# A third sum buffer, sum loads in SyncE's queue, and a VectorE subtraction for all late fourth sums, in an FFN made of seven-product blocks

## The chip, the cores and the metric

The kernel runs on one core of one Trainium2 chip. The metric is device time in microseconds (us) of one execution. The engines are named as in the profile: PE (TensorE), DVE (VectorE), ACT (ScalarE), POOL (GpSimd) and SP (SyncE, which here only issues DMAs).

## The reference

Two layers of a "macaron" encoder over 512 tokens and 16 learned meta tokens, model width 1024, FFN width 2816, float32. The change lies in the FFNs:

```python
def swiglu(x, w_gate, w_up, w_down):
    return (jax.nn.silu(x @ w_gate) * (x @ w_up)) @ w_down
...
for l in range(DEPTH):                       # DEPTH = 2
    h = h + 0.5 * swiglu(rmsnorm(h, norm_gains[l, 0]), ffn_w_gate[l, 0], ...)
    h = h + mixer(rmsnorm(h, norm_gains[l, 1]), ...)   # gated linear attention + softmax attention
    h = h + 0.5 * swiglu(rmsnorm(h, norm_gains[l, 2]), ffn_w_gate[l, 1], ...)
return rmsnorm(h, final_norm)[:, N_META:]
```

There are four FFNs in all, each with 11 pairs of 128 hidden features.

## The kernel before

**Products.** The matrix products of the FFNs are cut into 2 × 2 blocks and made by the scheme that takes seven products instead of eight. Every product is an "op" of one block of weights, 128 × 1024 (512 KB), against one half of the columns: 8 block tiles, each with three matmuls of 264 columns, so 24 matmuls. Three of the products (1, 2 and 4) use stored blocks, called 11, 12 and 22. Four (7, 6, 5 and 3) use sums of blocks that the kernel makes itself: s3 = 21 − 11, s2 = 22 + s3, s1 = 21 + 22, s4 = s2 − 12. The order of the products in a pair is 1, 2, 5, 6, 7, 4, 3 with changes where neighbours interleave.

**Splitting.** Every block is taken apart for the matmuls: ACT casts it to the short float format (`whi`, L259) and DVE subtracts that from the block for the rest (`wlo`, L260). The matmul needs both.

**Stages.** The 11 pairs (numbers 0 to 10) go in groups of 4, 4 and 3. A pair is the gate and up product (matmuls on line L566, the activation on L412, and L610, L620 that make its operands). After each of the first two groups stands a *down set*, two *quads* (numbered 11, 12 and 13, 14) that multiply the group's hidden values by `w_down` with the same seven products (matmuls L680), added into `h` by DVE (L688). A quad's product reads accumulators that an earlier addition must have emptied. The third group's down product is made in the plain way. The pairs that begin after a set are pair 4 and pair 8.

**Loads and sums.** The stored blocks are loaded by `block` (L193) into a pool of three raw buffers, in SP's queue. A sum begins in one of two pools: s3 and s4 in the "long" pool (three buffers), s2 and s1 in the "short" one (two buffers). s2 and s1 begin as a load of block 22 or 21 by the same `block`, but in POOL's queue, and then a DMA that accumulates (`add`, L203, always in POOL's queue) adds the other summand. s3 begins as a negated copy of block 11 by ACT (`negative`, L198). s4 is made in one of two ways: as a negated copy of block 12 by ACT (L198), to which POOL's queue accumulates s2; or, when `late` is true, by one DVE subtraction (L228) of block 12 from s2. For that the raw buffer of block 12 is kept (`self.kept`) until product 6's split has been made. `late` holds for pairs 2 to 10; the quads and the first two pairs take the first way.

**Order.** `make` prepares operands four ops ahead of PE and `fetch` loads nine ahead. The scheduler places the instructions of each engine by its own estimate of times; on the chip each engine, and each DMA queue's issuing engine, then goes through its list in order and waits at every entry for its semaphores.

Of the kernel before, what the change touches and what calls it, by code (L numbers as in the profile page):

```python
# [143 lines left out]
NPAIR = FF // P // 2  # L144
# [21 lines left out]
class Weights:  # L166
# [21 lines left out]
    def block(self, f, i, name, pool=None, tag="raw"):  # L188

        w = (pool or self.raw).tile([P, SLAB], F32, tag=tag, name=f"w{name}_{f[0]}{f[1]}_{i}")  # L190
        first = f + (i, name) == (0, 0, 0, "11")
        for a in np.split(np.arange(SLAB), 2 if first else 1):
            (self.nc.gpsimd if pool else self.nc.sync).dma_start(w[:, a[0] : a[-1] + 1], self.dram(f, i, name)[:, a[0] : a[-1] + 1])  # L193
        return w

    def negative(self, f, i, name, w):
# [8 lines left out]
    def sums(self, f, i, product, w):  # L205


        got = self.summed
        if product == "1":
            s3 = self.negative(f, i, "s3", w)  # L210
            self.add(s3, self.dram(f, i, "21"))
            s2 = self.block(f, i, "22", self.short, "wsb")
            self.add(s2, s3)
            got[f, i, "7"], got[f, i, "6"] = s3, s2
        if product == "12"[(f, i) in OPENING]:
            s1 = self.block(f, i, "21", self.short, "wsb")
            self.add(s1, self.dram(f, i, "22"))
            got[f, i, "5"] = s1
        late = 2 <= i < NPAIR
        if product == "2" and not late:  # L220
            s4 = self.negative(f, i, "s4", w)
            self.add(s4, got[f, i, "6"])
            got[f, i, "3"] = s4
        if product == "2" and late:
            self.kept = w
        if product == "6" and late:
            s4 = self.long.tile([P, SLAB], F32, tag="wsa", name=f"s4_{f[0]}{f[1]}_{i}")
            self.nc.vector.tensor_tensor(s4, w, self.kept, ALU.subtract)  # L228
            got[f, i, "3"] = s4
# [67 lines left out]
def build(tc, ctx, xt, wts, win, par, w2, const, umask, out):  # L297
# [17 lines left out]
    def open_pools(side, psum=(), **bufs):  # L315
        made[0] += 1
        out = {}
        for n, b in bufs.items():
            space = dict(space=bass.MemoryType.PSUM) if n in psum else dict(side=side)
            out[n] = tc.alloc_tile_pool(name=f"{n}_{made[0]}", bufs=b, reuse_waits="tile", **space)  # L320
        slots.update(out)
        return out
# [218 lines left out]
    def ffn(l, f, norm, done, following):  # L541

        x, rs, up, n = norm.x, None, None, live[0]
        w = n // 2
        pools = open_pools("left", psum=("s2",), c=4, s2=2)
        made, hid, sums, raw, sets = {}, {}, {}, {}, {}
        risen = iter(range(KC))

# [540 lines left out]
        norm.pools = open_pools("right", **{"x": dict(x=16), "xc": dict(xc=8)}[kind])  # L1089

    def block_pools():
        pools = open_pools("left", wsa=3, wsb=2)
        W.long, W.short = pools["wsa"], pools["wsb"]
        return pools

# [89 lines left out]
    def finish_chunk(c):  # L1185
        fin.square(c)
        gain(c, slice(0, SEQ))

    def ending(sums, operand, rs):

        table("abs_reciprocal_sqrt_and_small")
# [44 lines left out]
    first = Norm(G_NORM)  # L1236
    operand_pools(first, "xc")
    bp = [block_pools()]
    nc.sync.dma_start(h(1), xt[:, 1])
    first.pair(0)  # L1240
# [15 lines left out]
    for l in range(DEPTH):  # L1256
        a, b, c = norms[3 * l : 3 * l + 3]
        ffn(l, 0, a, b.chunk, lambda: operand_pools(b, "x"))
        close_pools(bp.pop())
        mixer(l, b, c.chunk_of_pair, lambda: (operand_pools(c, "xc"), bp.append(block_pools())))  # L1260
        if l < DEPTH - 1:
            d = norms[3 * l + 3]
            ffn(l, 1, c, d.pair_of, lambda: operand_pools(d, "xc"))
        else:
            ffn(l, 1, c, None, lambda: None)
# [72 lines left out]
```

## Time and profile before

| what | value |
|---|---|
| runs of the kernel | 2270.09, 2262.52, 2267.75 us; median 2267.75 |
| the profiled execution | 2280.39 us, its span 2278.6 us |
| mean granted clock of TensorE | 0.989 |
| busy in the span | PE 2188.9 us, DVE 1685.8, ACT 1262.7, POOL 246.1 |
| the four FFNs | about 0 to 405, 797 to 1145, 1142 to 1548, 1914 to 2279 us |
| DMA issues by L193 on POOL | 120, 576 ns of the engine each |
| DMA issues by L203 on POOL | `s<-win` 60, `w<-s` 60, `w<-win` 60, `s<-w` 24 |

A timeline row gives the start, the duration, engine, line, operation, what it writes and reads, and in brackets the idle time before it with what ended that. In the chain of waits a row is a piece of the chain that ended last: start, duration, and who held it. `w` stands for a block or short sum, `s` for a long sum, `win` for the stored blocks in memory, `ss` for an accumulator. A row of the waits names who waited for whom, the time in all, how often, and the longest.

### The profile page before, as it was taken

The page shows a single profiled execution, that of the slowest core. Times are in us where ns is not written, and L with a number is a line of the kernel's source. Part 1 is how long each engine was busy: PE and PEld are TensorE (multiplying, and loading weights), DVE is VectorE, ACT ScalarE, POOL GpSimd, SP SyncE. Part 2 cuts the span into 40 slices and gives each one's busy share as a digit, 9 for nine tenths or more (in the row PEclk, how much of TensorE's full clock was granted, in tenths as well). Part 3 has the DMA queues.
Part 4 walks back from the last instruction along what each step waited for, and adds up shares of the span by engine and source line. Part 5 has one row for each costly group of instructions (what it writes and reads, how often), then busy time and mean ns, then how long its engine had stood idle before and what let it go on. Part 6 is the DMA issues. An engine that isn't in the chain of part 4 may idle for free.

```text
span 2278.6 us, 40100 instructions
## 1 busy us (share of the span) xinstructions
PE 2188.9 (96%) x16506; PEld 2088.3 (92%) x16506; DVE 1685.8 (74%) x2607; ACT 1262.7 (55%) x1831; POOL 246.1 (11%) x328
## 2 busy tenths in 40 slices
PE   6989999999999999999999899999999999999998
PEld 6989999989999999998999898998888888999997
DVE  7776867586886678667788768575878767786867
ACT  7545545354785565454575455454547846555553
POOL 1211110000000011111012111100000001121110
PEclk9999999999999999999999999999999999999999
DMA  8877873212113477777668777832121135887871
GB/s 241 217 198 185 203 195 106 77 54 66 47 38 112 129 189 187 204 192 202 175 148 208 201 193 178 201 114 86 56 74 47 47 121 136 216 213 213 204 204 65
DMA packets 94951, 338.68 MB, mean 149 GB/s; under 512 B 10544, under 2 KB 12976, under 8 KB 94768
## 3 DMA queue, kind: packets, MB, share of 16 engines
q0 software_dynamic: 46656, 169.89, 33.9%
q1 hardware_dynamic: 46160, 163.73, 21.2%
q8 instruction: 130, 2.13, 0.4%
q10 hardware_dynamic: 1952, 2.50, 0.3%
q14 instruction: 53, 0.43, 0.1%
HBM read 289.94 MB, written 2.10 MB: 128 GB/s over the span
## 4 chain that ended last, share of the span: by engine, by line
PE 60%; DMA 13%; DVE 12%; issue 8%; ACT 6%; POOL 1%; SPq 0%; DVEq 0%; POOLq 0%; ACTq 0%
PE ss L566 24%; PE mm L433 14%; DMA w<-win 10%; PE ss L433 9%; PE ss L680 4%; DVE wlo L260 3%; PE sm L433 2%; DMA w<-s 2%; ACT whi L259 1%; PE sm L1041 1%; DMA s<-w 1%; PE ss L1016 1%; POOL w L203 1%; ACT s L198 1%; PE sm L1057 1%
## 5 line engine op out<-in xcount | busy, mean ns | idle before, releaser
L566 PE MATMUL ss<-xc,whi 128*128 128x264 f32 (+1 forms) x4928 | 905.6, 285 | 25.6 <-ACT whi L259 13.4
L566 PEld LDWEIGHTS ss<-xc,whi 128*128 128x128 f32 x4928 | 767.1, 189 | 30.8 <-ACT whi L259 14.3
L566 PE MATMUL ss<-xc,wlo 128*128 128x264 f32 (+1 forms) x2464 | 702.1, 285 | 3.7 <-DVE wlo L260 3.7
L260 DVE TENSOR_TENSOR wlo<-w,whi 128x1024 fp32r<-128x1024 f32 (+1 forms) x301 | 365.5, 1217 | 155.6 <-ACT whi L259 155.4
L566 PEld LDWEIGHTS ss<-xc,wlo 128*128 128x128 f32 x2464 | 466.3, 189 | 5.8 <-DVE wlo L260 5.8
L259 ACT CAST whi<-w 128x1024 fp32r<-128x1024 f32 (+1 forms) x301 | 313.0, 1047 | 143.1 <-DMA w<-win 34.0
L433 PE MATMUL mm<-x,whi 128*128 128x264 f32 (+1 forms) x1712 | 385.3, 315 | 0.0
L433 PEld LDWEIGHTS mm<-x,whi 128*128 128x128 f32 x1712 | 279.2, 189 | 16.5 <-issue 1.0
L680 PE MATMUL ss<-g,whi 128*128 128x264 f32 (+1 forms) x1280 | 250.9, 294 | 29.2 <-DVE h L688 17.2
L433 PE MATMUL mm<-x,wlo 128*128 128x264 f32 (+1 forms) x856 | 266.7, 316 | 0.0
L680 PEld LDWEIGHTS ss<-g,whi 128*128 128x128 f32 x1280 | 206.8, 196 | 35.9 <-ACT whi L259 19.5
L259 ACT CAST whi<-raw 128x1024 fp32r<-128x1024 f32 x126 | 132.1, 1049 | 164.4 <-PE mm L433 103.0
L570 ACT COPY c<-ss 128x528 f32<-128x528 f32 (+1 forms) x132 | 78.5, 595 | 224.3 <-PE ss L566 224.1
L260 DVE TENSOR_TENSOR wlo<-raw,whi 128x1024 fp32r<-128x1024 f32 x126 | 153.9, 1222 | 59.3 <-ACT whi L259 58.5
L680 PE MATMUL ss<-g,wlo 128*128 128x264 f32 (+1 forms) x640 | 186.1, 291 | 0.7 <-DVE wlo L260 0.7
L193 POOL DMA_DIRECT2D w<-win x120 | 69.1, 576 | 1079.9 <-DVE x L422 731.2
L260 DVE TENSOR_TENSOR wlo<-s,whi 128x1024 fp32r<-128x1024 f32 x120 | 146.5, 1221 | 43.5 <-ACT whi L259 43.4
L433 PEld LDWEIGHTS mm<-x,wlo 128*128 128x128 f32 x856 | 160.1, 189 | 8.5 <-issue 0.7
L433 PE MATMUL ss<-g,whi 128*128 128x264 f32 (+2 forms) x900 | 166.2, 299 | 0.0
L259 ACT CAST whi<-s 128x1024 fp32r<-128x1024 f32 x120 | 126.1, 1051 | 22.7 <-PE ss L680 15.3
L433 PEld LDWEIGHTS ss<-g,whi 128*128 128x128 f32 x900 | 131.7, 188 | 5.3
L680 PEld LDWEIGHTS ss<-g,wlo 128*128 128x128 f32 x640 | 125.3, 196 | 1.0 <-DVE wlo L260 1.0
(266 smaller groups left out, 3430.8 us busy)
## 6 DMA issues: line engine op xcount, KB each, us to landing
w<-win POOLq DMA_DIRECT2D x180, 512.0 KB, 6.1
w<-win SPq DMA_DIRECT2D x179, 512.0 KB, 5.4
raw<-wts SPq DMA_DIRECT2D x126, 512.0 KB, 3.3
s<-win POOLq DMA_DIRECT2D x60, 512.0 KB, 7.6
w<-s POOLq DMA_DIRECT2D x60, 512.0 KB, 5.2
s<-w POOLq DMA_DIRECT2D x24, 512.0 KB, 7.7
h<-xt SPq DMA_DIRECT2D x3, 528.0 KB, 8.7
out<-h ACTq DMA_DIRECT2D x4, 256.0 KB, 2.3
```

The source lines that it names most:

```text
L193: (self.nc.gpsimd if pool else self.nc.sync).dma_start(w[:, a[0] : a[-1] + 1], self.dram(f, i, name)[:, a[0] : a[-1] + 1])
L198: self.nc.scalar.activation(t, w, AF.Copy, scale=-1.0)
L203: self.nc.gpsimd.dma_start(t, src, accum_op=ALU.add)
L259: nc.scalar.copy(hi[:, cs], w[:, cs])
L260: nc.vector.tensor_tensor(lo[:, cs], w[:, cs], hi[:, cs].bitcast(F32), ALU.subtract)
L433: TE.matmul(acc.half[i][:width], lhs, rhs[:, acc.spans[i]], start=first, stop=last)
L566: TE.matmul(acc[:, j], a[:, j, k], b[:, at], start=bool(begin and k == 0 and i == 0), stop=k == len(x) - 1 and i == 2, skip_group_check=no ...
L570: W.behind = S.copy(part(st, q), acc).ins
L680: TE.matmul(acc[:, j], a[:, j, k], xs[b][:, k], start=bool(begin and k == 0 and i == 0), stop=k == 3 and i == 2, skip_group_check=not begin)
L1016: TE.matmul(s[:n, i, :HF], lhs, kh[:, hs], start=True, stop=False)
L1041: TE.transpose(tp[:, j * w + u * n : j * w + (u + 1) * n], pr[:n, (2 * c2 + j) * P : (2 * c2 + j + 1) * P], ident[:n, :n])
L1057: TE.matmul(o[:, :w], vw, ph, start=i == 0, stop=False)
```

## The change

It has three edits:

1. `block` loads into the short pool go in SP's queue too: 120 loads, 60 of block 22 (s2) and 60 of block 21 (s1). The accumulating DMAs stay in POOL's queue.
2. `late` holds for the quads too. In the 16 quads (four per FFN) s4 is made by the DVE subtraction, 52 in all instead of 36; 16 negations on ACT and 16 accumulations in POOL's queue go away (24 `s<-w` become 8). The quads' raw block 12 is kept until its s2 has been split.
3. The short pool has three buffers instead of two.

```diff
     def block(self, f, i, name, pool=None, tag="raw"):
         ...
         for a in np.split(np.arange(SLAB), 2 if first else 1):
-            (self.nc.gpsimd if pool else self.nc.sync).dma_start(w[:, a[0] : a[-1] + 1], self.dram(f, i, name)[:, a[0] : a[-1] + 1])
+            self.nc.sync.dma_start(w[:, a[0] : a[-1] + 1], self.dram(f, i, name)[:, a[0] : a[-1] + 1])
         return w
...
     def sums(self, f, i, product, w):
         ...
-        late = 2 <= i < NPAIR
+        late = 2 <= i
...
     def block_pools():
-        pools = open_pools("left", wsa=3, wsb=2)
+        pools = open_pools("left", wsa=3, wsb=3)
         W.long, W.short = pools["wsa"], pools["wsb"]
         return pools
```

## The prediction

> **What bounds the kernel now.** I read the page's busy times first, then the waits of TensorE, then the six worst places in the timelines and in the chain of waits. TensorE is busy nearly all the time; the changed lines belong to POOL, SP and VectorE, so they can only be worth something where PE waits for them:
>
> ```profile
> PE 2188.9 (96%) x16506; PEld 2088.3 (92%) x16506; DVE 1685.8 (74%) x2607; ACT 1262.7 (55%) x1831; POOL 246.1 (11%) x328
> ...
> PE ss L680 <- DVE h L688: 18.5, 8, 4.3
> PE ss L566 <- ACT whi L259: 13.4, 4, 8.9
> ```
>
> The span is 2278.6 us, so PE is idle for 2278.6 − 2188.9 = 89.7 us. The longest item (us, times, longest) is a matmul of a down set, L680, that waits for a VectorE addition into `h`, L688. In the window of the last FFN alone the same item is small, so six of the eight waits, worth 18.5 − 1.3 = 17.2 us, are in the three FFNs before it (two sets each):
>
> ```profile
> PE ss L680 <- DVE h L688: 1.3, 2, 0.7
> ```
>
> What holds that addition is seen in the VectorE and PE timelines at the end of the first down set:
>
> ```profile
> 149.68 1.23 DVE L260 TENSOR_TENSOR wlo<-w,whi 128x1024 fp32r<-128x1024 f32 x1 [0.30 <-ACT whi L259]
> 156.80 1.23 DVE L228 TENSOR_TENSOR s<-w,w 128x1024 f32<-128x1024 f32 x1 [5.89 <-DMA w<-s]
> 157.94 0.70 DVE L688 TENSOR_TENSOR h<-h,ss 128x528 f32<-128x528 f32 x1
> ...
> 154.22 0.28 PE L680 MATMUL ss<-g,wlo 128*128 128x264 f32 x1
> 158.79 0.78 PE L680 MATMUL ss<-g,whi 128*128 128x264 f32 x2 [4.29 <-DVE h L688]
> ```
>
> VectorE takes its instructions in order. The subtraction L228 that makes the fourth sum of the next pair stands ahead of the addition, and it waits 5.89 us for its operand, the second sum (a DMA that accumulates, `w<-s`). PE's last product of the set needs the buffer that the addition reads, and stands still for 4.29 us. The wait also costs the clock. The window table puts the granted clock at 0.52 between 157 and 164, and the chain of waits gives the run of 24 matmuls behind each of the six stalls, beside a run at full speed:
>
> ```profile
> 157.00:164.00 7.00, 5.21 (x24) 5.24 (x25) 4.53 (x5) 0.87 (x1) 0.56 (x1) 0.52 1.02 252
> ...
> 158.79 5.37 PE ss L680 x24
> 164.16 10.86 PE ss L566 x89
> 292.31 4.70 PE ss L680 x24
> 930.29 4.47 PE ss L680 x24
> 1064.42 4.68 PE ss L680 x24
> 1299.78 4.68 PE ss L680 x24
> 1437.16 4.57 PE ss L680 x24
> ```
>
> 10.86/89 = 0.122 us a matmul; 24 take 2.93 us. The six runs take 28.47 us against 6 × 2.93 = 17.58: 10.9 us more. A set's end therefore costs 17.2 + 10.9 = 28.1 us in all six.
>
> **The change, part by part.** First the order on VectorE. Built, the changed program has at all eight set ends: `wlo` of the next pair's product 1, the addition L688, then L228. That order exists in the trace already, in the last FFN:
>
> ```profile
> 2041.49 0.69 DVE L688 TENSOR_TENSOR h<-h,ss 128x512 f32<-128x512 f32 x1 [0.60 <-PE ss L680]
> 2044.96 1.23 DVE L228 TENSOR_TENSOR s<-w,w 128x1024 f32<-128x1024 f32 x1 [2.78 <-DMA w<-s]
> ...
> 2029.87 17.24 PE ss L680 x143
> ```
>
> L228 still waits 2.78 us for its DMA there, yet PE runs on: 143 matmuls in 17.24 us, 0.121 each. So the stall goes, unless what stands behind L228 is late next. Behind it on VectorE is `wlo` of product 2. In the first set PE would end product 3 at 154.22 + 0.28 = 154.50, then run two products of 2.93 to 160.36. L228 takes until 157.94 − 156.80 = 1.14 before its successor starts, and `wlo` 1.22: L228 must start by 160.36 − 1.14 − 1.22 = 158.0. Before, PE restarts 158.79 − 156.80 = 1.99 after L228 starts, so the spare time of a set end is about 158.0 − 154.5 + 1.99 − stall = 5.5 − stall: 1.2 us at the first, and 5.5 − (17.2 − 4.29)/5 = 2.9 in the mean of the other five.
>
> Will the second sum come as early as now? The chain ahead of the first end, the release of its raw buffer in the changed kernel, and the issue groups (median us to landing):
>
> ```profile
> 133.18 7.60 DMA w<-win
> ...
> 140.86 1.07 ACT s L198
> ...
> 142.33 0.19 POOL s L203
> ...
> 143.49 5.83 DMA w<-win
> ...
> 149.37 0.63 issue
> 149.99 6.73 DMA w<-s
> ...
> 135.87 1.22 DVE L260 TENSOR_TENSOR wlo<-w,whi 128x1024 fp32r<-128x1024 f32 x1
> ...
> w<-win SPq DMA_DIRECT2D x179, 512.0 KB, 5.4
> s<-win POOLq DMA_DIRECT2D x60, 512.0 KB, 7.6
> w<-s POOLq DMA_DIRECT2D x60, 512.0 KB, 5.2
> ```
>
> Two effects oppose each other. The load at 143.49 is the second sum's own; it lands at 149.32, and the accumulation starts after it. With a third buffer and SP's queue it is issued some 20 us sooner and binds no longer. But the raw block of product 1 was issued at 133.18 because L198 had freed block 12; that block is now kept for the new subtraction, and the raw load waits for the `wlo` that ends at 137.09, 3.9 us later. From there, with medians: 137.1 + 5.4 + 0.1 + 1.47 (140.86 to 142.33) + 7.6 + 0.6 + 5.2 = 157.5, against 156.72 now. With 5.2 for the middle accumulation it is 155.1; with the chain's own 7.60 and 6.73 it is 161.2. I take 1.3 us for the first end (half way from 157.5 to the high end is 159.3, past 158.0), and none for the others, whose spare 2.9 holds the 0.8. Set ends: −28.1 + 1.3 = −26.8, bounds −28.1 and, at the high end, −11 (worked out below).
>
> By the Trainium skill, "TensorE: Matmul & The Clock Gate", Part 1, the clock falls to half after an idle window of about 3.4 us. By that rule alone only the first stall would cost the clock, and the set ends would hold 17.2 + 2.4 = 19.6 us. The trace disagrees: after 2.21 us of idle time (292.31) the 24 matmuls took 4.70, so the sum stays with the rows.
>
> The opening of the first FFN is the other place with a second sum that comes late:
>
> ```profile
> 37.77 6.64 DMA w<-win
> ...
> 45.08 4.84 DMA w<-s
> ...
> 51.04 0.80 PE L566 MATMUL ss<-xc,whi 128*128 128x264 f32 x2 [3.52 <-ACT whi L259]
> 52.30 0.59 PE L566 MATMUL ss<-xc,wlo 128*128 128x264 f32 x1 [0.46 <-DVE wlo L260]
> 52.30 7.77 PE ss L566 x41
> ...
> 30.25 1.22 POOL L203 DMA_DIRECT2D s<-win  x1
> ```
>
> That load had to wait for one of two buffers; now it goes in the first microseconds. What binds instead is the third sum's accumulation, issued at 30.25; at the 7.6 median it lands at 37.9, and the whole 3.52 + 0.46 + (7.77 − 41 × 0.122 = 2.77) = 6.75 us could go. The DMA engines are full in the opening, and one transfer sooner is another later, so the bounds are 0 and −6.75 (a loss is not excluded, but the moved load carries the bytes it carried), and I take half: −3.4.
>
> The sixteen new subtractions, and those next to them:
>
> ```profile
> L228 DVE TENSOR_TENSOR s<-w,w 128x1024 f32<-128x1024 f32 x36 | 43.9, 1221 | 39.5 <-DMA w<-s 39.5
> ...
> 110.72 1.23 DVE L260 TENSOR_TENSOR wlo<-w,whi 128x1024 fp32r<-128x1024 f32 x1 [2.64 <-ACT whi L259]
> ...
> 101.79 0.90 POOL L203 DMA_DIRECT2D w<-s  x1 [6.50 <-DMA w<-win]
> ```
>
> 16 × 1.22 = 19.5 us of VectorE. In the first three FFNs the first quad's stands in the hole of 2.64 us before 110.72, provided its second sum is there: its accumulation was issued at 101.79, and 5.2 later is 107.0. So 1.22 fits in 2.64, at no cost. In the last FFN it stands in the chain from the activation to the next operand, with no hole: 2 × 1.22 = 2.4 us if all shows, 0 if PE has work; I take 1.2. The second quad's eight stand between a `wlo` and the next, cost nothing while those are ahead of PE, and 8 × 1.22 = 9.8 at worst. Sixteen negations on ACT and sixteen accumulations leave POOL's queue; neither row is on PE's path at a set end, so nothing, save less DMA traffic. Moving 120 loads off POOL takes issue time from an engine that is 11% busy: nothing.
>
> Sum: −26.8 − 3.4 + 1.2 = −29.0 us. The profiled execution took 2280.39 us; by it the changed kernel takes 2251.4. That execution lies 0.56% over the median of the three runs, 2267.75; by the median the time is 2267.75 − 29 = **2239 us**.
>
> **Rivals.** *The wait moves on (A).* The kept block delays the second sum to the high end, 4.5 us later than now (161.2 against 156.72). The first end then waits 3.3 us on product 2, each of the others 4.5 − 2.9 = 1.6: 11.3, and some 1 us of half clock at each, 6: 17 of the 28.1 stay, the set ends bring −11, the whole −11 − 3.4 + 1.2 = −13: 2254 us. For it: the deadline of the first end is only 0.5 us off at medians. Against it: the medians, and POOL's queue with fewer requests.
>
> *Slower (B): the sums land late because their loads share SP's queue with the raw blocks.* An SP transfer takes 5.4 now; with 120 more among 179, every sum lands L later. At the ends the cost is 6L − (1.2 + 5 × 2.9 = 15.7) + 10.9 of clock; at the eight first-quad subtractions, which VectorE now waits for in order, 8 × (L − 2.5): the sum is there at 107.0 and the hole leaves until 110.72 − 1.22 = 109.5. Together 14L − 24.8, which equals the 30 us to be gained at L = 3.9. At L = 5 the net is +15: 2283 us. For it: in the first window quoted above the DMA engines are at 1.02 of their time. Against it: the bytes are the same, and the loads start earlier than they did. The Trainium skill, "DMA: Bandwidth & Descriptors", section "Queues, rings and completion order", says an engine goes round the queue rows packet by packet; that would let SP's longer row get a smaller part for each transfer than two rows get together. Only the run can show the size.
>
> *No change (C):* the addition goes free, but the last product of a set and the two behind it find their `whi` late, since ACT's casts wait for the same DMAs. Six ends keep their stall in another name; the opening alone remains: 2264 us. Against it: the last FFN's set ends.
>
> **How the numbers follow.** A difference of 0.3% (6.8 us) is about what a measurement of this kernel can tell from no change. Forecast, from 2228 (all of 28.1 and 6.75 and 3.7 for the scatter of the runs, which spread by 7.6) to 2248: 0.58; A, 2248 to 2261: 0.20; C, up to 2274.5: 0.09; B: 0.13. Faster 0.78, same 0.09, slower 0.13. The range is 2228 to 2261: it leaves out C and B, 0.22, so I take it to 2263.
>
> **What would show it.** Right: in the waits of PE the item L680 for L688 falls from 18.5 to under 4; the chain has no x24 run over 3.5 us at the six ends; the gap at 51 us shrinks. A shows as L566 waiting for `wlo` L260 at the set ends; B as SP's `w<-win` median above 6.5 and VectorE waiting at the first-quad L228 for `w<-s`; C as L680 or L566 waiting for ACT `whi` there. A time above 2261 would make the forecast wrong.

## The result and the profile after

The changed kernel took 2243.84 us (median of four runs, 2242.97 to 2245.97) against 2267.18 of the kernel before in the same comparison: a ratio of 0.990, 95% interval 0.9882 to 0.9919, or 23.3 us. Measured a second time beside other kernels the ratio was 0.9884 (0.9858 to 0.991). Forecast were 29.0 us less and 2239, range 2228 to 2263. The forecast was right in its sign and range. Its sum, however, misses a gain and nearly all of a loss, which stand against each other.

The profiled execution took 2244.17 us, its span 2242.4. It is 36.2 us shorter than the profiled execution before, 13 us more than the medians differ by. The kernel before scatters widely (2264 to 2283 us in the later comparisons), its profiled execution lies high among its runs, and the changed kernel's lies at its median. So the traces tell here where time went, and the comparisons how much.

The page after, and the waits that answer to those shown of before:

```profile
PE 2175.8 (97%) x16506; PEld 2076.8 (93%) x16506; DVE 1700.5 (76%) x2623; ACT 1247.2 (56%) x1815; POOL 164.7 (7%) x192
...
PE ss L566 <- ACT c L570: 17.5, 12, 5.1
PE ss L566 <- ACT whi L259: 7.4, 2, 7.2
PE ss L680 <- DVE h L688: 3.1, 2, 1.6
PE ss L680 <- ACT g L641: 1.4, 2, 1.2
...
DVE s L228 <- DMA w<-s: 46.9, 8, 6.7
```

The waits for L688 fell from 18.5 to 3.1 us, and the two that are left are in the last FFN: the six set ends have none. VectorE, however, waits longer for the second sum than it did (39.5 before). Both are seen at the first set end, in the timelines of VectorE and PE:

```profile
142.90 0.70 DVE L688 TENSOR_TENSOR h<-h,ss 128x528 f32<-128x528 f32 x1 [0.70 <-PE ss L680]
150.31 1.23 DVE L228 TENSOR_TENSOR s<-w,w 128x1024 f32<-128x1024 f32 x1 [6.71 <-DMA w<-s]
151.46 1.22 DVE L260 TENSOR_TENSOR wlo<-w,whi 128x1024 fp32r<-128x1024 f32 x1
...
152.73 0.39 PE L566 MATMUL ss<-xc,wlo 128*128 128x264 f32 x1 [0.83 <-DVE wlo L260]
```

L688 goes ahead, L228 waits 6.71 us behind it, and PE meets only `wlo` of product 2, 0.83 us late: the deadline of the prediction was missed by about that.

Where the time went is read from PE rows that both traces have, before and after in turn: the same short wait early in the second, third and last FFN, and the last wait at the end:

```profile
822.20 0.51 PE L566 MATMUL ss<-xc,whi 128*128 128x264 f32 x2 [1.50 <-ACT c L570]
1189.22 0.51 PE L566 MATMUL ss<-xc,whi 128*128 128x264 f32 x2 [0.73 <-ACT c L570]
1942.53 0.50 PE L566 MATMUL ss<-xc,whi 128*128 128x256 f32 x2 [1.59 <-ACT c L570]
2269.52 0.70 PE L1208 MATMUL ss<-t,const 128*128 128x256 f32 x2 [0.80 <-ACT t L1204]
```

```profile
801.07 0.52 PE L566 MATMUL ss<-xc,whi 128*128 128x264 f32 x2 [1.50 <-ACT c L570]
1156.26 0.52 PE L566 MATMUL ss<-xc,whi 128*128 128x264 f32 x2 [0.73 <-ACT c L570]
1890.20 0.50 PE L566 MATMUL ss<-xc,whi 128*128 128x256 f32 x2 [1.60 <-ACT c L570]
2233.26 0.70 PE L1208 MATMUL ss<-t,const 128*128 128x256 f32 x2 [0.80 <-ACT t L1204]
```

The differences are 21.1, 33.0, 52.3 and 36.3 us. The stretches of the first three FFNs won 52.3 us; the last gave 16.1 back. What it lost is on PE and on ACT:

```profile
1950.97 0.50 PE L566 MATMUL ss<-xc,whi 128*128 128x256 f32 x2 [4.51 <-ACT c L570]
2083.52 0.80 PE L566 MATMUL ss<-xc,whi 128*128 128x256 f32 x2 [5.11 <-ACT c L570]
...
1948.65 1.06 ACT L198 ACTIVATE s<-w 128x1024 f32<-128x1024 f32 x1 [6.00 <-DMA w<-win]
1949.62 0.81 ACT L641 CAST c<-g 128x768 fp32r<-128x768 f32 x1
1950.34 0.58 ACT L570 COPY c<-ss 128x512 f32<-128x512 f32 x1
```

PE waits for the accumulator copy L570 (17.5 us in all, 9.9 before). On ACT the copy stands behind the negation L198 of the second quad's raw block, which waits 6.00 us for its load. In the trace of before the order is the same and the load is there sooner:

```profile
1997.85 1.06 ACT L198 ACTIVATE s<-w 128x1024 f32<-128x1024 f32 x1 [2.85 <-DMA w<-win]
1999.54 0.58 ACT L570 COPY c<-ss 128x512 f32<-128x512 f32 x1
2000.17 0.50 PE L566 MATMUL ss<-xc,whi 128*128 128x256 f32 x2 [1.36 <-ACT c L570]
```

### The profile page after: what moved, and what is told of

Read it like the earlier page. It is cut to its first block, busy times and chain, and to the rows that moved or that the text cites. A ratio compares the mean times of both kernels' runs of the same rounds, so it can differ in the third digit from the quotient of the medians.

```text
span 2242.4 us, 40104 instructions
## 1 busy us (share of the span) xinstructions
PE 2175.8 (97%) x16506; PEld 2076.8 (93%) x16506; DVE 1700.5 (76%) x2623; ACT 1247.2 (56%) x1815; POOL 164.7 (7%) x192
## 5 line engine op out<-in xcount | busy, mean ns | idle before, releaser
L566 PE MATMUL ss<-xc,whi 128*128 128x264 f32 (+1 forms) x4928 | 907.0, 286 | 28.1 <-ACT c L570 17.5
L680 PE MATMUL ss<-g,whi 128*128 128x264 f32 (+1 forms) x1280 | 239.7, 286 | 5.7 <-DVE h L688 3.1
L680 PEld LDWEIGHTS ss<-g,whi 128*128 128x128 f32 x1280 | 198.6, 188 | 10.3 <-ACT whi L259 3.5
L680 PE MATMUL ss<-g,wlo 128*128 128x264 f32 (+1 forms) x640 | 181.2, 283 | 0.0
L570 ACT COPY c<-ss 128x528 f32<-128x528 f32 (+1 forms) x132 | 78.2, 593 | 142.7 <-PE ss L566 142.6
L259 ACT CAST whi<-s 128x1024 fp32r<-128x1024 f32 x120 | 126.1, 1051 | 21.1 <-ACT g L641 7.4
L433 PEld LDWEIGHTS ss<-g,whi 128*128 128x128 f32 x900 | 131.7, 188 | 5.2
L203 POOL DMA_DIRECT2D w<-win x60 | 56.6, 944 | 982.0 <-DVE wlo L260 395.8
L198 ACT ACTIVATE s<-w 128x1024 f32<-128x1024 f32 x68 | 71.8, 1058 | 93.7 <-DMA w<-win 83.9
```

The source lines that it names most:

```text
L198: self.nc.scalar.activation(t, w, AF.Copy, scale=-1.0)
L203: self.nc.gpsimd.dma_start(t, src, accum_op=ALU.add)
L259: nc.scalar.copy(hi[:, cs], w[:, cs])
L433: TE.matmul(acc.half[i][:width], lhs, rhs[:, acc.spans[i]], start=first, stop=last)
L566: TE.matmul(acc[:, j], a[:, j, k], b[:, at], start=bool(begin and k == 0 and i == 0), stop=k == len(x) - 1 and i == 2, skip_group_check=no ...
L570: W.behind = S.copy(part(st, q), acc).ins
```

## The experiments

Four kernels ran in the first comparison, four in the second, three in the third; each comparison had a chip of its own, and every ratio is to the kernel before on the same chip. Theory ORDER was the prediction's: the place of L688 ahead of L228 is what frees the set ends. Its rival SUPPLY: the second sums are loaded earlier.

**The quads' subtraction alone.**

```diff
-        late = 2 <= i < NPAIR
+        late = 2 <= i
```

> The kernel before with one edit: the quads' fourth sum by the DVE subtraction (late = 2 <= i). Theory ORDER (the gain at the set ends hangs on the place of L688 ahead of L228 in VectorE's list, and this edit alone moves it): the PE waits of L680 for L688 fall from 18.5 to under 4, no run of 24 matmuls over 3.5 us at the six ends, the opening keeps its 3.5 us wait at 51 us; 2240 to 2246 us. Rival SUPPLY (the stalls went because the second sums' loads start earlier, by SP's queue and the third buffer): the raw block is kept here and nothing is earlier, so the second sum is some 4 us late, PE waits for wlo at the set ends instead; 2258 to 2272 us.

Measured: 2258.63 us, ratio 0.994 (0.9919 to 0.996). Waits of this kernel:

```profile
PE ss L566 <- DVE wlo L260: 8.7, 15, 1.1
PE ss L680 <- DVE wlo L260: 4.6, 6, 1.0
PE ss L680 <- DVE h L688: 3.1, 2, 1.6
...
DVE s L228 <- DMA w<-s: 50.3, 9, 6.7
```

The mark of ORDER is there: L688 at 3.1 with VectorE waiting 50.3 us. The time is SUPPLY's, at the edge of its range. The gain of the set ends is partly spent again: PE waits 13.3 us for `wlo` (4.4 before), 4.6 of them within the quads, and the last FFN is longer (below). One expectation missed: the wait of 3.5 us at 51 us in the opening is not in this trace, although no edit touches the opening; a wait of 2.4 us for `whi` stands at 18 us instead.

**Queue and third buffer, without the subtraction.**

```diff
-            (self.nc.gpsimd if pool else self.nc.sync).dma_start(...)
+            self.nc.sync.dma_start(...)
-        pools = open_pools("left", wsa=3, wsb=2)
+        pools = open_pools("left", wsa=3, wsb=3)
```

> The changed kernel without the edit of late: loads of sums in SP's queue and the third short buffer only. ORDER: VectorE keeps L228 ahead of L688 at six set ends, so the waits for L688 stay; they shrink only as far as the second sum lands earlier (its load no longer gates, about 1.3 us an end), and the opening's 6.7 us go: 2252 to 2262 us. SUPPLY: the second sum is there before L228 and the six stalls go: 2236 to 2246 us.

Measured: 2241.32 us, 0.9864 (0.9842 to 0.9886), and 0.9869 (0.9846 to 0.9892) the second time.

```profile
PE ss L566 <- ACT c L570: 16.8, 11, 5.2
DVE s L228 <- DMA w<-s: 8.0, 7, 3.5
PE ss L680 <- DVE h L688: 3.3, 3, 1.9
```

SUPPLY's forecast came true: with the old order, L228 waits little (8.0 against 39.5), so L688 behind it is on time at five of the six set ends; at the first PE still waits 1.9 us. ORDER as the only cause is refuted.

**The order alone.** In the kernel before, for pairs 4 and 8, L228 is put behind the addition of the set's product 7 (lines move by two to four: L230 is L228, L690 is L688).

```diff
+            with self.tc.issue_after(self.added) if self.added and i in (4, 8) else nullcontext():
-            self.nc.vector.tensor_tensor(s4, w, self.kept, ALU.subtract)
+                self.nc.vector.tensor_tensor(s4, w, self.kept, ALU.subtract)
...
+                add = V.tensor_tensor(to, to, acc, ALU.add)
+                if (dq, c) == (1, "7"):
+                    W.added = add.ins
```

> The kernel before with nothing changed but the order on VectorE: for pairs 4 and 8 the L228 subtraction is put behind the addition L688 of the set's product 7. Queues, buffers and the negations of before stay. ORDER: L228 waits as long as before, PE does not; 28 us less in the sum, 2238 to 2244 us. SUPPLY: PE stops at the next operand behind L228 instead, waiting for wlo; 2255 to 2268 us.

Measured: 2251.03 us, 0.9905 (0.9878 to 0.9933), runs from 2242.68 to 2257.36. The time lies between the two forecasts; the waits are ORDER's:

```profile
DVE s L230 <- DMA w<-s: 25.0, 11, 4.4
PE ss L682 <- DVE h L690: 1.3, 2, 0.7
```

Nothing is loaded earlier by design, and the six stalls go. So there are two remedies, and either is enough for these stalls: put the addition first, or have the sum there. The trace is that of the fastest of the six runs, 2242.68 us; where the others lose up to 15 us more is not shown. That VectorE's wait fell to 25.0 too was not expected, and no run shows why.

**The negation later, in the last FFN.** The changed kernel, with L198 of the second quad's block (and the sums that follow from it) issued five products later; lines move by up to ten.

```diff
+        with self.tc.issue_after(self.behind) if f == (1, 1) and i in (12, 14) else nullcontext():
+            self.nc.scalar.activation(t, w, AF.Copy, scale=-1.0)
...
+                    if load[0] == (1, 1) and load[1] in (12, 14):
+                        self.later.append((self.uses + 5, load, self.raws[self.fetched]))
+                    else:
+                        self.sums(*load, self.raws[self.fetched])
...
+        while self.later and self.later[0][0] <= self.uses:
+            _, load, w = self.later.pop(0)
+            self.sums(*load, w)
```

> The changed kernel; in the last FFN alone ACT's negation L198 of the second quad's block (and with it that quad's s3, s2) is issued five products later, behind the accumulator copy L570 and the casts that PE needs first. Theory CROWD (in the last FFN the sums' loads now stand ahead of this raw block, it lands some 3 us later, and ACT's list holds the negation ahead of the copy): the two PE waits of 4.5 and 5.1 us for L570 shrink to under 1.5 each, with the half clock behind them; 8 us less than the changed kernel, 2233 to 2238 us. Rival: the waits move on to the casts behind it, or the VectorE subtraction in that chain is what costs; 2241 to 2247 us.

Measured: 2238.16 us, 0.985 (0.9824 to 0.9876).

```profile
PE ss L575 <- ACT c L579: 7.9, 12, 1.6
PE ss L689 <- DVE h L697: 3.1, 2, 1.6
```

CROWD holds, with the time at the very edge of its range: the waits for the copy fall from 17.5 to 7.9, the longest from 5.1 to 1.6, and the last FFN takes 330.2 us from its landmark (the wait of 1.6 us for L570) to the end instead of 343.1. The edit holds back the quad's sums along with the negation, so it does not tell ACT's order from the loads that crowd. The two waits for L688 in the last FFN stay; the subtraction alone has them too.

**The queue alone, and the buffer alone.**

> The kernel before with one edit: the sums' loads in SP's queue, two short buffers, late as before. Theory OVERLAP (an earlier second sum and the order on VectorE are two remedies for the same six stalls; the earlier sum needs both a free buffer and a queue that does not hold the load behind POOL's accumulation of the third sum): the load is free of POOL's list but still waits for one of two buffers, and raw blocks wait behind it in SP's list; the L688 waits stay above 10 us, 2254 to 2268 us. Rival QUEUE (the queue alone brings the second sum forward): L228 waits under 15 us for its DMA in all, 2238 to 2248.

> The kernel before with one edit: three short buffers, loads of sums still in POOL's queue, late as before. OVERLAP: the load has its buffer but stands behind the third sum's accumulation in POOL's list, which waits for ACT's negation; at a set end the second sum is at most 1 or 2 us earlier, the L688 waits stay above 10 us; the opening gains part of its 6.7 us; 2254 to 2266 us. Rival BUFFER (the buffer alone does it): L228 waits under 15 us in all, 2238 to 2248.

Measured: the queue 2254.04 us, 0.9919 (0.9894 to 0.9945); the buffer 2250.51, 0.9903 (0.9877 to 0.9928). The waits, the queue first:

```profile
DVE s L228 <- DMA w<-s: 33.6, 12, 4.0
PE ss L680 <- DVE h L688: 12.0, 8, 2.5
PE ss L566 <- ACT whi L259: 7.3, 1, 7.3
```

```profile
DVE s L228 <- DMA w<-s: 4.6, 4, 1.7
PE ss L680 <- DVE h L688: 1.3, 2, 0.7
PE ss L566 <- ACT whi L259: 14.9, 4, 9.4
```

OVERLAP was right on the queue, at the edge of its range, and wrong on the buffer: rival BUFFER's waits came true, and the time lies between the two forecasts. The third buffer alone takes the wait out of the set ends, although the loads stand in POOL's list; the queue alone takes out a third of it, and shortens the opening (`whi` 7.3 against 13.4 before; with the buffer 14.9). The windows of the first 60 us, before, queue, buffer and changed kernel in turn:

```profile
0.00:60.00 60.00, 42.12 (x264) 38.89 (x265) 43.09 (x69) 44.03 (x68) 11.59 (x19) 0.94 0.89 244
```

```profile
0.00:60.00 60.00, 47.55 (x330) 44.88 (x331) 49.57 (x82) 48.60 (x74) 10.89 (x16) 1.00 0.98 278
```

```profile
0.00:60.00 60.00, 41.85 (x281) 39.14 (x282) 44.01 (x71) 44.99 (x69) 12.96 (x22) 1.00 0.93 254
```

```profile
0.00:60.00 60.00, 46.15 (x320) 43.12 (x321) 48.37 (x80) 47.61 (x73) 10.88 (x16) 1.00 0.98 277
```

With the queue PE has done 330 matmuls by 60 us, with the buffer 281. Kernels that leave the opening as it was had 264 (before), 286 (subtraction alone) and 308 (order alone), so the opening scatters by 44 matmuls, 5.4 us, between executions. Over all traces the two groups stay apart: the five with the sums' loads in POOL's queue have 264 to 308, in the mean 286, the eight with them in SP's have 314 to 330, in the mean 323. The difference of the means is 37 matmuls, 4.5 us.

**Two edits at a time, with the subtraction.**

> The sums' loads in SP's queue and the quads' DVE subtraction; two short buffers. Theory REMEDY (the third buffer alone takes the wait out of the set ends, the order that the subtraction brings does it too, the queue only shortens it; what is left of each after the other has done it is its own price): the queue alone left 12 us of L688 waits; the subtraction's order takes them away, so here the edit of late still pays: 0.987 to 0.991 of before, 2243 to 2252 us. Rival (the subtraction has a price of its own of 5 us or more wherever it is): 0.992 or more.

> The third short buffer and the quads' DVE subtraction; loads of sums in POOL's queue. REMEDY: the buffer had already taken the L688 waits away (1.3 us left), so the edit of late brings nothing here and costs its kept raw block and the waits for wlo: 0.990 to 0.994 of before, 2250 to 2260 us, level with or behind the buffer alone at 0.9903. Rival (the subtraction helps by itself, 16 negations and accumulations less): 0.988 or less.

> Queue and third buffer without the quads' subtraction, a second time, beside the other two on the same chip. REMEDY: the best of the three, 0.984 to 0.988 of before; the rival that the subtraction helps: behind queue and late.

Measured: queue and subtraction 2248.44 us, 0.9904 (0.9883 to 0.9926); buffer and subtraction 2252.65, 0.9927 (0.9905 to 0.9948); queue and buffer 2240.13, 0.9869. REMEDY's forecasts held in all three, with the first at the upper part of its range. The ratios, without and with the subtraction:

| | without | with | last FFN, us: without | with |
|---|---|---|---|---|
| neither | 1 | 0.994 | 327.0 | 334.7 |
| queue | 0.9919 | 0.9904 | 328.9 | 335.7 |
| buffer | 0.9903 | 0.9927 | 332.5 | 339.9 |
| both | 0.9864, 0.9869 | 0.990, 0.9884 | 335.7, 335.5 | 343.1, 342.1 |

(The last two columns go from the landmark wait of 1.6 us for L570 to the wait of 0.8 us for L1204 in each trace: before, 2269.52 − 1942.53 = 327.0.) The subtraction pays 0.6% where the set ends are not mended otherwise, 0.15% beside the queue, and with the buffer it is behind by 0.15 to 0.35%. Only the 0.6% was measured within one comparison; the others set ratios from different chips side by side, their intervals overlap, and no more can be said than that beside queue or buffer no gain clear of the scatter is seen. In the last FFN the subtraction costs some 7 us in all four rows.

**Queue, buffer, order and the later negation**, with the quads' sums as before:

> The loads in SP's queue and the third buffer, the quads' fourth sums as before (negation and accumulation), and two edits of order: L228 of pairs 4 and 8 behind the addition of the set's product 7, and in the last FFN ACT's negation of the second quad's block issued five products later. OVERLAP with CROWD: all three places are mended and the raw block is not kept; the set ends have no wait for L688 over 1 us, the two waits for L570 in the last FFN fall from 5 to under 1.6; 2228 to 2236 us, under the changed kernel with the late negation by up to 5. Rival: the DVE subtraction of the quads is worth something by itself (16 negations and 16 accumulations less); then this is slower than the changed kernel with the late negation, 2240 to 2246.

Measured: 2233.32 us, 0.9826 (0.98 to 0.9852), as OVERLAP and CROWD had it: the waits for L688 (L699 there) come to 1.3 us in all, and the longest for L570 (L581) is 1.6. It beats the kernel before, and the changed kernel beside it (2247.04) by 13.7 us. Its last FFN takes 329.4 us.

**The changed kernel again.**

> The changed kernel once more, beside the others on the same chip: 0.988 to 0.992 of before. By OVERLAP the quads' subtraction adds nothing once queue and buffer are there, so it is level with or up to 0.4% behind queue and buffer alone, which had 0.986; the rival that the subtraction helps would put it at 0.984 or less.

Measured: 2247.04 us, 0.9884, against 0.9864 and 0.9869 of queue and buffer alone in other comparisons; no help from the subtraction is seen once queue and buffer are there.

## Why the prediction was right, and where not

*What bounds the kernel, and the set ends (forecast −26.8).* Right. The six L688 waits are gone, the slow matmuls behind them too, and the 0.83 us at the first end stands for the 1.3 allowed there. The mechanism was right for the kernel as built: L688 ahead of L228, the second sum later than before, covered by two products. What the prediction did not see is that the third buffer by itself would have done as much at these ends. It argued that the raw block binds next. The late sum is seen only with the subtraction, which keeps the block: L228 waits 46.9 us with it, 8.0 without.

*The opening (−3.4, bounds 0 and −6.75).* Mis-sized in the trace: (320 − 264) × 0.122 = 6.8 us, the high end; by the means of all traces it is 4.5. The wait that the term was built on, 3.52 us at 51 us, does not hold from trace to trace: the subtraction alone and the order alone, whose edits do not touch the opening, do not have it. Nor is it borne out that a buffer was short there, as the prediction had it: with the third buffer alone the count of 281 lies within the scatter, and a wait of 4.7 us for `whi` stands at 21 us. It is the queue that raises the count. The DMA engines were not full either; their share of the first 60 us rose from 0.89 to 0.98. The first wait for `whi`, which no step had, is 8.9 to 10.3 us in the five traces with POOL's queue and 7.2 to 7.5 in the eight with SP's.

The Trainium skill, "DMA: Bandwidth & Descriptors", section "Issuing engines are not separate DMA queues", says that another issuing engine saves only issue time. The queue alone gave 0.8%, and POOL was only 11% busy. That need not contradict it: a load in POOL's list also waits behind what POOL itself waits for (6.50 us for a DMA in the row at 101.79), and of that the rule says nothing. A rival was not tested: the profile page lists POOL's queue as `software_dynamic` and SP's as `hardware_dynamic`, and before the change packets took 33.9% of the engines' span for 169.89 MB in the one and 21.2% for 163.73 MB in the other. POOL's queue holds the accumulations too, so it is open whether a plain load is faster in SP's queue.

*The operands of the sets (nothing).* This was missing. The waits of PE before for what L620, L641 and L642 make of the hidden values:

```profile
PE ss L680 <- ACT g L641: 8.1, 11, 1.7
PE ss L680 <- DVE g L620: 3.3, 2, 2.0
PE ss L680 <- DVE g L642: 2.4, 4, 0.7
```

After, L641 is at 1.4 us and the other two are not there: 12.4 us less, 10.9 of them ahead of the last FFN. Neither the queue alone (L641 10.1), the buffer alone (9.8), nor the subtraction alone (7.8) does it; queue and buffer leave 5.5, and the changed kernel 3.0 in its second trace. How the three add up here stays open.

*The last FFN (+1.2, bounds 0 and +2.4).* This is the step that failed, at 16.1 us: PE is idle 9.0 us longer there (17.9 against 8.9), and the rest is slower matmuls. Two things were taken for one. The subtraction in the chain of operands was priced by its own 1.2 us; alone it costs 7.7, of which the rows show the two L688 waits of 1.6 (0.7 before) and the `wlo` waits. And rival B was right in mechanism at a place it did not name: the sums' loads, issued earlier, crowd the raw block that ACT negates, and ACT's list holds the copy that PE needs behind it. That the loads crowd it is the reading of the runs: queue and buffer without the subtraction already make PE wait 5.2 us for the copy, but no run shows what holds the block. Queue (1.9), buffer (5.5) and subtraction (7.7) add up to 15.1 of the 16.1, yet they are not prices that stand by themselves. With the second quad's negation and sums five products later, 3.2 of the 16.1 are left (330.2 us), and the kernel that also drops the subtraction and has the order written out is only 0.8 us shorter there (329.4).

*The sum.* In the trace the set ends (28.1 − 0.83), the opening, the operands and the last FFN make −27.3 − 6.8 − 10.9 + 16.1 = −28.9 of −36.3. The other 7.4 us are not put down to a row; most lie between the landmarks of the third and the last FFN, where 19.3 us went and idle time accounts for 10.7. The medians say −23.3 and −26. That the forecast of −29.0 came near is luck in part: a missing gain and a missing loss of similar size stood against each other. The low end of the range is 1 us off its own working (2267.75 − 28.1 − 6.75 − 3.7 = 2229.2).

*Rivals.* A (the wait moves to `wlo`) appeared as 0.83 us at one end, and in the second trace of the changed kernel as 0.3 to 1.2 us at five, 2.9 in all. C did not occur. B's L of 5 us for every sum did not occur either: SP's `w<-win` took 5.2 at the median, 5.4 before.

## What to carry to other kernels

Where an in-order engine holds what the next engine needs behind an instruction that waits for a transfer, there are two cures, to change the order or to bring the transfer forward, and here their gains did not add: run each alone before building both. A load that is brought forward can take the place of one that was in time, so look on every engine's list for the next wait on a load and for what stands behind it. And where an edit flips an order as a side effect, try the order itself, written out: here that left out the subtraction and its cost in the last FFN.

## What the hardware showed that was not expected

Whether the matmuls behind a short stall run slower depends on more than the stall's length. In the kernel with the queue alone, the chain of waits has these runs of 24 at the six set ends, after stalls of 2.31, 1.21, 1.33, 1.02, 2.47 and 2.33 us:

```profile
148.82 4.68 PE ss L680 x24
...
280.51 3.16 PE ss L680 x24
...
913.67 3.16 PE ss L680 x24
...
1043.81 3.19 PE ss L680 x24
...
1277.01 3.16 PE ss L680 x24
...
1408.12 4.58 PE ss L680 x24
```

After 2.47 us the run went at nearly full speed (24 × 0.122 = 2.93), after 2.31 and 2.33 most of it at half. In the kernel with queue and subtraction a stall of 3.14 us cost no speed at all, the next 24 matmuls took 2.93 us:

```profile
2086.45 0.50 PE L566 MATMUL ss<-xc,whi 128*128 128x256 f32 x2 [3.14 <-ACT c L570]
```

And in the last FFN of the kernel before, the same pair of waits, 0.67 us for L688 and 0.9 for L642, comes twice: in the 10 us from 2016 on the granted clock is 1.00, in those from 2141 on 0.83. The Trainium skill, "TensorE: Matmul & The Clock Gate", Part 1, says that the window by which activity is watched runs freely, so that the point of change varies; these rows agree with that, though not with 3.4 us of idle time as the least that halves it.
